# A log-softmax that streams through SBUF: eight 25 KB buffers with one maximum per row, in place of four 50 KB buffers with a maximum per piece

## The chip, the core and the metric

The kernel runs on one core of one Trainium2 chip. The metric is the device time of one execution in microseconds (us). A core has engines that run on their own and meet by semaphores: TensorE (PE in the profile), VectorE (DVE), ScalarE (ACT), GpSimd (POOL) and SyncE (SP). The last one only issues transfers here. Data moves between the device memory (HBM) and the on-chip memory SBUF (128 partitions) by 16 DMA engines, which serve the transfers that SP and ACT issue. Each issuing engine has its own queue: q1 in the profile holds the loads that SP issues, q10 the stores that ACT issues.

## The reference

The input is 16 x 512 rows of 50,000 float32 numbers, so 8,192 rows and 1,638.4 MB; the output has the same size. For each row:

```python
max_x = np.max(x, axis=-1, keepdims=True)
shifted = x - max_x
log_sum_exp = np.log(np.sum(np.exp(shifted), axis=-1, keepdims=True))
return (shifted - log_sum_exp).astype(np.float32)
```

Every number is read once, the maximum and the sum of a whole row are needed before any of its outputs can be written, and every output is written once.

## The kernel before

A row lies on G = 4 neighbouring partitions, 12,500 numbers (50,000 bytes) on each, so a tile is 32 rows on 128 partitions, 6.4 MB. There are 256 tiles and NBUF = 4 buffers of 50,000 bytes per partition; tile after tile takes the next buffer. Each engine has its own program, a loop of 64 rounds over the four buffers, and nothing but semaphores orders the engines against each other. The helper `Count` holds the value that the next instruction is to wait for; its `settle` sets a semaphore back at the end of a round; `take` (L43) waits until all 16 parts of a transfer have landed.

**SP** issues the first four loads at once (L138). After that it waits until the store out of a buffer has landed, and issues the next load into this buffer (L142).

**DVE**, for each buffer in turn: waits for the load (L43). It takes the negated maximum of each of four pieces of 3,125 numbers (L153). It then brings the four to one number per partition (L160), and spreads the maximum of the 4 partitions of a row to all of them with two 32x32 transposes and two small operations (L164 to L179). It waits for ACT, multiplies the piece sums by their corrections (L183), waits for the logarithm, and writes `x + negmax - logsum` over the buffer (L186).

**ACT**, for each buffer: exponentials of each piece, shifted by the piece's own maximum, written to a dump in PSUM with the sum of each partition kept (L201), each as soon as DVE has that piece's maximum. Then the corrections exp(piece maximum - row maximum) (L209), the logarithm of the row's sum (L215), and the issue of the store when DVE has finished the buffer (L218).

**PE** adds the corrected sums over the 4 partitions of a row by a matrix of ones and zeros, four products of one column (L229). **POOL** makes this matrix once.

So one tile goes through load, DVE, ACT, PE, ACT, DVE, store. DVE and ACT finish with one tile before they begin the next; the loads and stores of the other three buffers run meanwhile.

Of the kernel before, what the change touches and what calls it, by code (L numbers as in the profile page):

```python
# [8 lines left out]
FP32 = mybir.dt.float32  # L9
ACT = mybir.ActivationFunctionType  # L10
ALU = mybir.AluOpType
AX = mybir.AxisListType.X

P = 128
SQ = 32

G = 4
R = P // G
EXP_C = 3125
NBUF = 4  # L20


class Count:
# [11 lines left out]
    def settle(self, engine):  # L35
        if self.seen:
            engine.wait_ge(self.sem, self.seen).then_inc(self.sem, -self.seen)
        self.seen = 0


def take(engine, sem):

    engine.wait_ge(sem, 16).then_inc(sem, -16)  # L43
# [3 lines left out]
def kernel(  # L47
# [8 lines left out]
    N, V = xf.shape  # L56
    W = V // G
    assert N % R == 0 and V % G == 0 and W % EXP_C == 0
    ntiles = N // R
    nexp = W // EXP_C  # L60
    assert ntiles % NBUF == 0 and ntiles >= 2 * NBUF

    rounds = ntiles // NBUF
    xq = xf.rearrange("(q j r) (g w) -> q j (r g) w", j=NBUF, r=R, g=G)
    oq = of.rearrange("(q j r) (g w) -> q j (r g) w", j=NBUF, r=R, g=G)

    data = ctx.enter_context(tc.tile_pool(name="data", bufs=1))
    stats = ctx.enter_context(tc.tile_pool(name="stats", bufs=1))
# [7 lines left out]

    ones = consts.tile([P, P], FP32)
    bufs = [data.tile([P, W], FP32, name=f"buf{j}") for j in range(NBUF)]
    dump = dump_pool.tile([P, EXP_C], FP32, name="dump")
    rowsum = sum_pool.tile([P, NBUF], FP32, name="rowsum")  # L80

    def each(shape, name):
        return [stats.tile(shape, FP32, name=f"{name}{j}") for j in range(NBUF)]

    negms, parts, scales, scaleds = (
        each([P, nexp], n) for n in ("negm", "part", "scale", "scaled")
    )
    negmaxs, logs = each([P, SQ], "negmax"), each([P, 1], "logsum")
    negp = stats.tile([P, 1], FP32, name="negp")
    allneg = stats.tile([P, SQ], FP32, name="allneg")  # L90
    rowneg = stats.tile([P, SQ // G], FP32, name="rowneg")
    spread = stats.tile([P, SQ], FP32, name="spread")


    ctx.enter_context(tc.tile_critical())  # L95
# [1 line left out]
    def sem(name):  # L97
        return ctx.enter_context(nc.semaphore(name))

    landed = [sem(f"landed{j}") for j in range(NBUF)]  # L100
    stored = [sem(f"stored{j}") for j in range(NBUF)]
    ready = sem("ones_ready")
    on_dve = Count(sem("on_dve"))
    on_act = Count(sem("on_act"))
    shifted = Count(sem("shifted"))
    agreed = Count(sem("agreed"))
    rescaled = Count(sem("rescaled"))
    summed = Count(sem("summed"))
    added = Count(sem("added"))
    logged = Count(sem("logged"))  # L110
    subtracted = Count(sem("subtracted"))


    def dram(a, q, j):
        if isinstance(q, int):
            return a[q, j]
        return a[bass.ds(q, 1), j].rearrange("o p w -> (o p) w")
# [3 lines left out]
    @block.gpsimd  # L121
    def _(gpsimd):

        ones3 = ones.rearrange("p (r g) -> p r g", g=G)
        gpsimd.memset(ones, 1.0).then_inc(ready)  # L125
        gpsimd.affine_select(  # L126
            out=ones3, in_=ones3, pattern=[[-G, R], [0, G]], base=0,
            channel_multiplier=1, compare_op=ALU.is_ge, fill=0.0,
        ).wait_op(ready, 1, "sem-ge").then_inc(ready)
        gpsimd.affine_select(  # L130
            out=ones3, in_=ones3, pattern=[[G, R], [0, G]], base=G - 1,
            channel_multiplier=-1, compare_op=ALU.is_ge, fill=0.0,
        ).wait_op(ready, 2, "sem-ge").then_inc(ready)
# [11 lines left out]

    @block.vector
    def _(vector):
        with vector.Fori(0, rounds):
            for j in range(NBUF):
                take(vector, landed[j])  # L150

                for c in range(nexp):
                    vector.tensor_reduce(  # L153
                        out=negms[j][:, c : c + 1],
                        in_=bufs[j][:, c * EXP_C : (c + 1) * EXP_C],
                        op=ALU.max, axis=AX, negate=True,
                    ).then_inc(shifted.sem if c < nexp - 1 else on_dve.sem)
                on_dve.next(vector.nop()).then_inc(shifted.sem)  # L158

                vector.tensor_reduce(  # L160
                    out=negp, in_=negms[j], op=ALU.min, axis=AX
                ).then_inc(on_dve.sem)
                on_dve.next(
                    vector.transpose(out=allneg, in_=negp.to_broadcast([P, SQ]))  # L164
                ).then_inc(on_dve.sem)
                on_dve.next(
                    vector.tensor_reduce(  # L167
                        out=rowneg, in_=allneg.rearrange("p (r g) -> p r g", g=G),
                        op=ALU.min, axis=AX,
                    )  # L170
                ).then_inc(on_dve.sem)
                on_dve.next(
                    vector.tensor_copy(  # L173
                        out=spread.rearrange("p (r g) -> p r g", g=G),
                        in_=rowneg[:, :, None].to_broadcast([P, SQ // G, G]),
                    )
                ).then_inc(on_dve.sem)
                on_dve.next(
                    vector.transpose(out=negmaxs[j], in_=spread)  # L179
                ).then_inc(agreed.sem)  # L180

                rescaled.next(
                    vector.tensor_mul(out=scaleds[j], in0=scales[j], in1=parts[j])  # L183
                ).then_inc(summed.sem)
                logged.next(
                    vector.tensor_scalar(  # L186
                        out=bufs[j], in0=bufs[j], scalar1=negmaxs[j][:, 0:1],
                        scalar2=logs[j], op0=ALU.add, op1=ALU.subtract,
                    )
                ).then_inc(subtracted.sem)  # L190
            for count in (on_dve, rescaled, logged):
                count.settle(vector)

    @block.scalar
    def _(scalar):
        nc.scalar.preload_act_table_set("natural_log_exp_and_others")  # L196
        with scalar.Fori(0, rounds) as q:
            for j in range(NBUF):
                for c in range(nexp):
                    shifted.next(  # L200
                        scalar.activation(  # L201
                            out=dump, in_=bufs[j][:, c * EXP_C : (c + 1) * EXP_C],
                            func=ACT.Exp, bias=negms[j][:, c : c + 1], scale=1.0,
                            accum_out=parts[j][:, c : c + 1],
                        )
                    ).then_inc(on_act.sem)
                    on_act.next(scalar.nop())  # L207
                agreed.next(
                    scalar.activation(  # L209
                        out=scales[j], in_=negms[j], func=ACT.Exp,  # L210
                        bias=negmaxs[j][:, 0:1], scale=-1.0,
                    )
                ).then_inc(rescaled.sem)
                added.next(
                    scalar.activation(out=logs[j], in_=rowsum[:, j : j + 1], func=ACT.Ln)  # L215
                ).then_inc(logged.sem)
                subtracted.next(
                    scalar.dma_start(out=dram(oq, q, j), in_=bufs[j])  # L218
                ).then_inc(stored[j], 16)
            for count in (on_act, shifted, agreed, added, subtracted):  # L220
                count.settle(scalar)

    @block.tensor
    def _(tensor):
        tensor.wait_ge(ready, 3)
        with tensor.Fori(0, rounds):
            for j in range(NBUF):
                for c in range(nexp):
                    ins = tensor.matmul(  # L229
                        rowsum[:, j : j + 1], ones, scaleds[j][:, c : c + 1],  # L230
                        start=c == 0, stop=c == nexp - 1,
                    )
                    if c == 0:
                        summed.next(ins)
                ins.then_inc(added.sem)
            summed.settle(tensor)


# [28 lines left out]
```

## Time and profile before

| what | value |
|---|---|
| time of three runs | 7587.72, 7589.31 and 7597.37 us; median 7589.31 |
| the profiled execution: its own time | 7589.31 us |
| its span, first to last instruction | 7587.6 us |
| DVE busy | 5440.0 us (72%) |
| ACT busy | 3184.7 us (42%) |
| PE busy | 478.0 us (6%) |
| moved by DMA | 3276.85 MB, mean 432 GB/s |
| a load, from issue to landing (median) | 44.1 us |
| a store, from issue to landing (median) | 47.7 us |

The profile page has a row of 40 digits for each engine: the share of each fortieth of the span in which it was busy, in tenths. The DMA row does the same for the mean of the 16 DMA engines, and a row of GB/s says what they moved. Packets are the single pieces that a DMA engine moves; here a data packet is one partition's line of a tile, and a packet of 4 bytes raises the semaphore at the end of a transfer's share on one DMA engine. The trace has a record of every packet, with its queue, size, start and duration. "Chain" on the page is the work followed back from the last instruction; it knows instructions and semaphores, and not the packets of a transfer. A window view gives, for a stretch of time, the busy time of every engine, and in its last two columns the DMA share and GB/s. The landing of a transfer comes when the last of its 16 shares is done.

### The profile page before, as it was taken

Reading aid. Unit: us, or ns where it says so; the run is one execution under the profiler, and the core shown is the slowest. Engines: PE = TensorE matmul, PEld = TensorE weight load, DVE = VectorE, ACT = ScalarE, POOL = GpSimd, SP = SyncE. Lnnn points to the kernel's source line nnn. Section 1 sums busy time; section 2 is a strip of 40 time slices with the busy share of each in tenths; the row PEclk is TensorE's granted clock in tenths of the full one; section 3 lists DMA queues with packets and bytes.
Section 4 is the critical chain, followed back from the end, with each engine's and each line's share of the span. In section 5 each row is a group of like instructions: output and inputs, shape, how many; then the busy total and the mean of one; then the engine's idle time right before and its main releaser. Section 6 shows DMA issues by size and latency. Waiting matters only on the chain. (4 is left out here: it accounts for less than half of the span.)

```text
span 7587.6 us, 14087 instructions
## 1 busy us (share of the span) xinstructions
PE 478.0 (6%) x2048; PEld 456.0 (6%) x2048; DVE 5440.0 (72%) x2816; ACT 3184.7 (42%) x2561; POOL 1.4 (0%) x7
## 2 busy tenths in 40 slices
PE   0000000000000000000000000000000000000000
PEld 0000000000000000000000000000000000000000
DVE  7777777777777777777777777777777777777776
ACT  4444344443444444344443444444344443444433
POOL 0000000000000000000000000000000000000000
DMA  9999999999999999999999999999999999999998
GB/s 415 434 433 434 434 434 433 434 434 433 434 434 434 433 433 434 433 434 434 434 433 434 434 433 434 434 434 433 434 434 433 433 434 434 434 432 433 433 433 382
DMA packets 73730, 3276.85 MB, mean 432 GB/s; under 512 B 8192, under 2 KB 8192, under 8 KB 8192
## 3 DMA queue, kind: packets, MB, share of 16 engines
q1 hardware_dynamic: 36864, 1638.42, 50.0%
q10 hardware_dynamic: 36864, 1638.42, 49.9%
q14 instruction: 2, 0.02, 0.0%
HBM read 1638.40 MB, written 1638.40 MB: 432 GB/s over the span
## 5 line engine op out<-in xcount | busy, mean ns | idle before, releaser
L201 ACT ACTIVATE dump<-buf,negm 128x3125 f32<-128x3125 f32 x1024 | 2937.2, 2868 | 3802.3 <-DVE negm L153 3704.9
L153 DVE TENSOR_REDUCE negm<-buf 128x1 f32<-128x3125 f32 x1024 | 3418.2, 3400 | 920.5 <-DVEq L43 920.5
L186 DVE TENSOR_SCALAR buf<-buf,negmax,logsum 128x12500 f32<-128x12500 f32 x256 | 1738.3, 6790 | 553.8 <-ACT logsum L215 553.8
L229 PE MATMUL rowsum<-scaled,ones 128*128 128x1 f32 x2048 | 478.0, 355 | 7084.5 <-DVE scaled L183 7084.5
L229 PEld LDWEIGHTS rowsum<-scaled,ones 128*128 128x128 f32 x2048 | 456.0, 328 | 7106.4 <-DVE scaled L183 7106.4
L183 DVE TENSOR_TENSOR scaled<-scale,part 128x4 f32<-128x4 f32 x256 | 41.7, 163 | 580.5 <-ACT scale L209 580.5
L215 ACT ACTIVATE logsum<-rowsum 128x1 f32<-128x1 f32 x256 | 43.8, 171 | 551.1 <-PE rowsum L229 551.1
L201 ACT ACTIVATION_READ_ACCUMULATOR dump<-buf,negm 128x1 f32 x1024 | 190.9, 186 | 0.0
L209 ACT ACTIVATE scale<-negm,negmax 128x4 f32<-128x4 f32 x256 | 76.1, 297 | 23.6
L160 DVE TENSOR_REDUCE negp<-negm 128x1 f32<-128x4 f32 x256 | 40.1, 157 | 39.2 <-DVE negm L153 39.2
L179 DVE STREAM_TRANSPOSE negmax<-spread 128x32 f32<-128x32 f32 x256 | 54.2, 212 | 8.9
L164 DVE STREAM_TRANSPOSE allneg<-negp 128x32 f32<-128x32 f32 x256 | 54.1, 211 | 8.9
L167 DVE TENSOR_REDUCE rowneg<-allneg 128x8 f32<-128x32 f32 x256 | 47.6, 186 | 8.9
L173 DVE COPY spread<-rowneg 128x32 f32<-128x32 f32 x256 | 46.3, 181 | 8.9
L196 ACT ACT_TABLE_LOAD x1 | 1.3, 1283 | 1.0 <-SPq L95 1.0
L126 POOL TENSOR_SCALAR_AFFINE_SELECT ones<-ones 128x128 f32<-128x128 f32 x1 | 0.5, 520 | 0.1
L130 POOL TENSOR_SCALAR_AFFINE_SELECT ones<-ones 128x128 f32<-128x128 f32 x1 | 0.5, 518 | 0.1
L125 POOL MEMSET ones<- 128x128 f32 x1 | 0.2, 205 | 0.5 <-SPq L95 0.5
L251 POOL MEMSET const-bfloat16-1.0<- 128x1 bf16 x1 | 0.1, 102 | 0.0
L251 POOL MEMSET const-uint8-127<- 128x1 uint8 x1 | 0.1, 102 | 0.0
L251 POOL MEMSET const-float32-0.0<- 128x1 f32 x1 | 0.1, 99 | 0.3 <-issue 0.3
L251 POOL MEMSET const-float32-1.0<- 128x1 f32 x1 | 0.1, 99 | 0.0
## 6 DMA issues: line engine op xcount, KB each, us to landing
buf<-in_x_dram SPq DMA_DIRECT2D x256, 6250.0 KB, 44.1
out_dram<-buf ACTq DMA_DIRECT2D x256, 6250.0 KB, 47.7
```

The source lines that it names most:

```text
L153: vector.tensor_reduce(out=negms[j][:, c : c + 1], in_=bufs[j][:, c * EXP_C : (c + 1) * EXP_C], op=ALU.max, axis=AX, negate=True,).then_in ...
L160: vector.tensor_reduce(out=negp, in_=negms[j], op=ALU.min, axis=AX).then_inc(on_dve.sem)
L164: vector.transpose(out=allneg, in_=negp.to_broadcast([P, SQ]))
L167: vector.tensor_reduce(out=rowneg, in_=allneg.rearrange("p (r g) -> p r g", g=G), op=ALU.min, axis=AX,)
L173: vector.tensor_copy(out=spread.rearrange("p (r g) -> p r g", g=G), in_=rowneg[:, :, None].to_broadcast([P, SQ // G, G]),)
L179: vector.transpose(out=negmaxs[j], in_=spread)
L183: vector.tensor_mul(out=scaleds[j], in0=scales[j], in1=parts[j])
L186: vector.tensor_scalar(out=bufs[j], in0=bufs[j], scalar1=negmaxs[j][:, 0:1], scalar2=logs[j], op0=ALU.add, op1=ALU.subtract,)
L201: scalar.activation(out=dump, in_=bufs[j][:, c * EXP_C : (c + 1) * EXP_C], func=ACT.Exp, bias=negms[j][:, c : c + 1], scale=1.0, accum_out ...
L209: scalar.activation(out=scales[j], in_=negms[j], func=ACT.Exp, bias=negmaxs[j][:, 0:1], scale=-1.0,)
L215: scalar.activation(out=logs[j], in_=rowsum[:, j : j + 1], func=ACT.Ln)
L229: ins = tensor.matmul(rowsum[:, j : j + 1], ones, scaleds[j][:, c : c + 1], start=c == 0, stop=c == nexp - 1,)
```

## The change

A row lies on G = 8 partitions, 6,250 numbers (25,000 bytes) on each; a tile is 16 rows, 3.2 MB; there are 512 tiles and eight buffers of 25,000 bytes per partition, so the SBUF in use by buffers is the same. SP and POOL keep their programs, with eight in place of four in the loops (and 64 rounds still).

DVE takes one maximum of all 6,250 numbers of a partition, then the two transposes and two small operations, and hands the row's maximum to ACT. ACT takes the exponentials of two pieces of 3,125 with the row's maximum, so no corrections are needed: L209 and L183 of before are gone, with the fold at L160. PE adds two columns in place of four.

The order within DVE and ACT is another one. DVE does the front of tile j (wait for its load, maximum, spread), and then the back of tile j - 1 (the subtraction). ACT does the front of tile j (exponentials, logarithm) and then issues the store of tile j - 1. The first round stands ahead of the loop, and the last back behind it.

```diff
-G = 4
+G = 8
-NBUF = 4
+NBUF = 8
...
     @block.vector
...
+        def front(j):
+            take(vector, landed[j])
+            vector.reduce_max(out=pmax, in_=bufs[j], axis=AX).then_inc(on_dve.sem)
+
+            on_dve.next(
+                vector.transpose(out=allmax, in_=pmax.to_broadcast([P, SQ]))
+            ).then_inc(on_dve.sem)
...
+            on_dve.next(vector.transpose(out=shift[j], in_=spread)).then_inc(shifted.sem)
+
+        def back(j):
+            logged.next(
+                vector.tensor_scalar(
+                    out=bufs[j], in0=bufs[j], scalar1=shift[j][:, 0:1], scalar2=logs[j],
+                    op0=ALU.add, op1=ALU.subtract,
+                )
+            ).then_inc(subtracted.sem)
...
+        with vector.Fori(1, rounds):
+            for j in range(NBUF):
+                front(j)
+                back((j - 1) % NBUF)
+            settle()
+        back(NBUF - 1)
...
     @block.scalar
...
+        def front(j):
+            for c in range(nexp):
+                ins = scalar.activation(
+                    out=dump, in_=bufs[j][:, c * EXP_C : (c + 1) * EXP_C], func=ACT.Exp,
+                    bias=shift[j][:, 0:1], scale=1.0, accum_out=parts[j][:, c : c + 1],
+                )
+                (on_act if c else shifted).next(ins)
+                ins.then_inc(on_act.sem if c < nexp - 1 else summed.sem)
+            added.next(
+                scalar.activation(out=logs[j], in_=rowsum[:, j : j + 1], func=ACT.Ln)
+            ).then_inc(logged.sem)
+
+        def back(q, j):
+            subtracted.next(
+                scalar.dma_start(out=dram(oq, q, j), in_=bufs[j])
+            ).then_inc(stored[j], 16)
...
+        with scalar.Fori(1, rounds) as q:
+            last = q - 1
+            for j in range(NBUF):
+                front(j)
+                back(q if j else last, (j - 1) % NBUF)
+            settle()
+        back(rounds - 1, NBUF - 1)
```

More of the change, by code (lines that the diff above doesn't have):

```diff
@@ L78 @@
     bufs = [data.tile([P, W], FP32, name=f"buf{j}") for j in range(NBUF)]
+    shift = [stats.tile([P, SQ], FP32, name=f"negmax{j}") for j in range(NBUF)]
+    logs = [stats.tile([P, 1], FP32, name=f"logsum{j}") for j in range(NBUF)]
+    parts = [stats.tile([P, nexp], FP32, name=f"part{j}") for j in range(NBUF)]
+    pmax = stats.tile([P, 1], FP32, name="pmax")
+    allmax = stats.tile([P, SQ], FP32, name="allmax")
+    rowmax = stats.tile([P, SQ // G], FP32, name="rowmax")
+    spread = stats.tile([P, SQ], FP32, name="spread")
     dump = dump_pool.tile([P, EXP_C], FP32, name="dump")
     rowsum = sum_pool.tile([P, NBUF], FP32, name="rowsum")
[L82 to L92, printed above, removed]
     ctx.enter_context(tc.tile_critical())
@@ L105 @@
     shifted = Count(sem("shifted"))
-    agreed = Count(sem("agreed"))
-    rescaled = Count(sem("rescaled"))
     summed = Count(sem("summed"))
@@ L147, in _ @@
     def _(vector):
-        with vector.Fori(0, rounds):
-            for j in range(NBUF):
[L150 to L192, printed above, removed]
@@ new lines, in front @@
+        def front(j):
[4 more added lines that the diff above has]
+            ).then_inc(on_dve.sem)
+            on_dve.next(
+                vector.tensor_reduce(
+                    out=rowmax, in_=allmax.rearrange("p (r g) -> p r g", g=G),
+                    op=ALU.max, axis=AX, negate=True,
+                )
+            ).then_inc(on_dve.sem)
+            on_dve.next(
+                vector.tensor_copy(
+                    out=spread.rearrange("p (r g) -> p r g", g=G),
+                    in_=rowmax[:, :, None].to_broadcast([P, SQ // G, G]),
+                )
+            ).then_inc(on_dve.sem)
+            on_dve.next(vector.transpose(out=shift[j], in_=spread)).then_inc(shifted.sem)
@@ new lines, in back, with settle @@
+        def back(j):
[3 more added lines that the diff above has]
+                    op0=ALU.add, op1=ALU.subtract,
+                )
+            ).then_inc(subtracted.sem)
+        def settle():
+            on_dve.settle(vector)
+            logged.settle(vector)
+        for j in range(NBUF):
+            front(j)
+            if j:
+                back(j - 1)
+        settle()
@@ L194, in _ @@
+        with vector.Fori(1, rounds):
+            for j in range(NBUF):
+                front(j)
+                back((j - 1) % NBUF)
+            settle()
+        back(NBUF - 1)
     @block.scalar
     def _(scalar):
-        nc.scalar.preload_act_table_set("natural_log_exp_and_others")
-        with scalar.Fori(0, rounds) as q:
-            for j in range(NBUF):
[L199 to L221, printed above, removed]
@@ new lines, in front @@
+        def front(j):
[3 more added lines that the diff above has]
+                    bias=shift[j][:, 0:1], scale=1.0, accum_out=parts[j][:, c : c + 1],
+                )
+                (on_act if c else shifted).next(ins)
[3 more added lines that the diff above has]
+            ).then_inc(logged.sem)
@@ new lines, in back, with settle @@
+        def back(q, j):
+            subtracted.next(
+                scalar.dma_start(out=dram(oq, q, j), in_=bufs[j])
+            ).then_inc(stored[j], 16)
+        def settle():
+            for count in (on_act, shifted, added, subtracted):
+                count.settle(scalar)
+        nc.scalar.preload_act_table_set("natural_log_exp_and_others")
+        for j in range(NBUF):
+            front(j)
+            if j:
+                back(0, j - 1)
+        settle()
+        with scalar.Fori(1, rounds) as q:
+            last = q - 1
+            for j in range(NBUF):
+                front(j)
+                back(q if j else last, (j - 1) % NBUF)
+            settle()
@@ L223, in _, with add @@
+        back(rounds - 1, NBUF - 1)
     @block.tensor
     def _(tensor):
+        def add(j):
+            for c in range(nexp):
+                ins = tensor.matmul(
+                    rowsum[:, j : j + 1], ones, parts[j][:, c : c + 1],
+                    start=c == 0, stop=c == nexp - 1,
+                )
+                if c == 0:
+                    summed.next(ins)
+            ins.then_inc(added.sem)
         tensor.wait_ge(ready, 3)
@@ L227, in _ @@
             for j in range(NBUF):
[L228 to L235, printed above, removed]
+                add(j)
             summed.settle(tensor)
```

## The prediction, made before the result was known

> **What bounds the kernel now.** I read the page's DMA rows first, because DVE, the busiest engine, stands at 72%.
>
> ```profile
> DMA  9999999999999999999999999999999999999998
> ...
> DMA packets 73730, 3276.85 MB, mean 432 GB/s; under 512 B 8192, under 2 KB 8192, under 8 KB 8192
> ...
> q1 hardware_dynamic: 36864, 1638.42, 50.0%
> q10 hardware_dynamic: 36864, 1638.42, 49.9%
> ```
>
> Loads and stores together fill 99.9% of the 16 DMA engines. A queue has 256 x 128 = 32,768 data packets of 50,000 bytes and 256 x 16 = 4,096 of 4 bytes. So the kernel is bound by how fast DMA engines work through packets, and engine work matters only where it lets them run dry. The windows show where they do:
>
> ```profile
> 2000.00:3000.00 1000.00, 63.48 (x272) 60.56 (x272) 719.95 (x369) 418.23 (x337) 0.00 (x0) 1.00 1.00 434
> ...
> 7555.00:7560.00 5.00, 0.00 (x0) 0.00 (x0) 2.84 (x6) 4.59 (x4) 0.00 (x0) 1.00 0.07 30
> 7560.00:7565.00 5.00, 1.87 (x8) 1.78 (x8) 2.44 (x2) 0.47 (x2) 0.00 (x0) 1.00 0.05 20
> 7565.00:7570.00 5.00, 0.00 (x0) 0.00 (x0) 4.51 (x1) 0.00 (x0) 0.00 (x0) 1.00 0.00 0
> 7570.00:7575.00 5.00, 0.00 (x0) 0.00 (x0) 0.00 (x0) 0.00 (x0) 0.00 (x0) 1.00 1.12 480
> ```
>
> The last two columns are DMA share and GB/s. In the middle nothing is idle; at the end DMA waits for the last tile's arithmetic. A share of 0.05 is one engine of 16 (1/16 = 0.06): one lags. The timeline of DVE has that last tile:
>
> ```profile
> 7543.54 13.35 DVE L153 TENSOR_REDUCE negm<-buf 128x1 f32<-128x3125 f32 x4 [3.61 <-DVEq L43]
> ...
> 7562.72 6.79 DVE L186 TENSOR_SCALAR buf<-buf,negmax,logsum 128x12500 f32<-128x12500 f32 x1 [2.16 <-ACT logsum L215]
> ```
>
> The packet records give prices. 63,862 of the 65,536 data packets take under 1849 ns (nearly all 1847); every 4-byte packet takes 9. Inside a transfer the next packet starts 1843 to 1844 ns after the last, so neighbours overlap by some 3.5 ns; with a 4-byte packet between them it is 1849 to 1850, so that one costs 6.
>
> The lagging engine: at tile 12 its load lands 2.7 us after the median engine's, at tile 180 11.4 us, so it loses 8.7 us / 168 = 52 ns per tile. Around 2000 us its long packets (1.89 us) start at 2028.81, 2058.39, 2087.97, one per tile, each spanning SP's next load issue (2029.29, 2058.77, 2088.30). It is always last, so it sets the end.
>
> Its time must add up to the span: first packet at 2.05; 512 transfers x (8 x 1843.5 + 6 ns = 14.754 us) = 7554.0; lag 256 x 52 ns = 13.3; dry from 7565.25 (its last packet of tile 254) to 7570.38 (the last store's first packet) = 5.1; 2.3 from the last packet at 7585.3 to the end. That is 7576.8; the other 10.8 us I put on the first 100 us, where 166 of the 305 packets over 1.9 us lie.
>
> **The change part by part.**
>
> *Packets half as long: the largest term.* A line through 4 bytes/9 ns and 50,000 bytes/1847 ns has 0.03676 ns per byte and 9 ns fixed. A 25,000-byte packet then takes 9 + 919 = 928 ns, less 3.5 overlap 924.5. A transfer's share on one engine is 8 x 924.5 + 6 = 7.402 us, and 1,024 of them are 7579.6 against 7554.0: **+25.6 us**. From below: were nothing fixed per packet, only 512 more semaphore packets of 6 ns remain, +3.1. From above: no overlap and 9 ns for each, 4,096 x 9 + 512 x 9 = +41.5. I take 25.6, as both rows give it.
>
> The Trainium skill (DMA: Bandwidth & Descriptors, "Why small descriptors are slow (HBM only)") has about 3 cycles fixed per packet. At the 850 MHz that its section "Where 436 GB/s comes from" gives, that is an estimated 3.5 ns, 4,096 x 3.5 = 14.5 us, and the sum below would come out 11 us lower. The same page ("Anatomy of one DMA") speaks louder against the change: about 2.0 us fixed per DMA, by which 512 more would cost an estimated 1,024 us if nothing covered them. The packets of this trace follow each other across transfers at 1.85 us with no such hole, so I take none of it.
>
> *Twice as many load issues.* If the 52 ns hang on an issue, they double: 256 x 52 = **+13.3 us**; if on bytes or time, 0. I take 13.3, since the long packets lie on the issues.
>
> *Arithmetic, beside DMA.* DVE: from 3398 ns for 3,125 numbers and 157 for 4 (L160), 1.04 ns each; 6,250 take 6.64 us. The spread from 7557.23 to 7558.13 is 0.9, the subtraction half of 6.79 to that plus 0.16, so 3.4 to 3.55: 11.1 us a tile. ACT has two exponentials with read-out (2.87 + 0.19 each), the wait for PE (half of 1.87) and the logarithm (0.17), about 7.4. DMA needs 14.8 us per tile. The fold, the corrections, L183 and two of PE's products go; they were hidden too: nothing.
>
> *The new wait.* DVE does back(j-1) after front(j), so a finished tile waits for the next load to land; behind DVE's wait stands that subtraction, behind ACT's exponentials stands the store, and SP waits for the store to issue a load. From landing to store issue: 14.8 + 7.6 (front) + 7.4 = 29.8 us, against 26.0 before (7543.54 to 7569.54). It is two of eight buffers; 8 x 14.8 - 29.8 = 88.6 us remain for load plus store, against 44.1 + 47.7 = 91.8. Both queues stay about three transfers deep: nothing. If the cover were gone: see the third rival.
>
> *The end.* After the last landing L, the store before last is issued at L + 7.6 + 7.4 = L + 15, the last one 3.5 later. Before, the lagging engine had stores until L + 21.8 (7543.4 to 7565.25). With as much left it doesn't run dry: **-5.1 us**. With nothing left, 15 us dry: +10.
>
> *The beginning.* The first load is half as long and the first store is issued near 33.5 us (two fronts of DVE after a landing near 11, then ACT's 7.4) instead of 45.38, so loads resume before the first ones run out. Of the 10.8 us that may save none (the slow packets come from the first mixing of reads and writes) or all. I take half, **-5 us**.
>
> **Sum:** 7587.6 + 25.6 + 13.3 - 5.1 - 5 = 7616.4 of span; with the 1.7 between this execution's span and its own time (7589.31, which is also the median) 7618 us, 0.38% slower. This kernel's runs tell about 0.2%, 15 us, from no change.
>
> **The rivals.** *Lag by time* (chance 0.22): the lag doesn't double. 7618 - 13.3 = 7605, on the edge of the 15 us. For it: the lagging engine may simply be slow.
>
> *No fixed cost per packet* (0.13; the one on the other side): packets go by bytes alone, and the shorter ends decide. 7589.3 + 3.1 - 5.1 - 5 to -10.8 = 7576 to 7582. It decides if a packet's fixed cost is under (10.1 - 3.1) / 4,096 = 1.7 ns and the lag stays. For it: 3.5 of the 9 ns overlap already; against it: the 5.5 that don't.
>
> *The store's wait starves the queues* (0.05): each us by which load plus store need more than the 88.6 costs 1/8 us per tile, 64 us in all. Against it: a store alone in its queue, the last one, took 7587.6 - 7569.54 = 18 us for twice the bytes.
>
> *Dearer small packets* (0.12): the full 9 ns or more for starts that lie otherwise in memory: 7618 + 16 = 7634 and, at 15 ns, 7660.
>
> *The forecast's own case* has 0.48. That the change does not do what it says has no room: the shapes are set by two constants.
>
> **How the numbers follow.** Slower by over 0.2% means above 7604.5: the forecast's case nearly whole, half of the lag rival, the two dear ones: 0.74. Faster means below 7574: the end of the second rival, 0.04. Within: 0.22. Range 7588 to 7642: it leaves out most of the second rival and the dear ones' upper parts.
>
> **What would show it.** Right: DMA share 1.00 and a rate near 432 GB/s in the middle windows (3.2 MB x 2 / 14.8 us), packets of 928 ns, a lag growing by 50 ns per tile, no dry window before the last store. Wrong: packets of 924 ns or less (second rival), a lag that ends near 13 us (first), shares under 1.00 in the middle (third), packets over 935 (fourth).

## The result and the profile after

The changed kernel takes 7618.68 us (median of six runs, 7617.30 to 7620.36), the kernel before 7589.23 us (median of six, 7587.59 to 7597.37). The ratio is 1.0036 with a 95% interval of 1.0023 to 1.0049: 29 us slower, beyond what these runs scatter. Runs more than 1.5% above the fastest of their kernel, two of loads_in_two and one of before_no_pe, are left out of the times given below. The prediction was 7618 us. The profiled execution of the changed kernel took 7619.4 us with a span of 7617.7, so 30.1 us more span than before.

The page of the changed kernel, its DMA rows:

```profile
span 7617.7 us, 14954 instructions
...
DMA  9999999999999999999999999999999999999998
GB/s 424 432 433 432 432 432 432 433 432 432 432 433 433 432 432 432 433 432 432 432 432 433 432 432 432 433 433 432 431 432 433 432 432 432 432 432 432 431 430 366
DMA packets 147459, 3276.88 MB, mean 430 GB/s; under 512 B 16385, under 2 KB 16385, under 8 KB 16385
...
q1 hardware_dynamic: 73728, 1638.43, 50.0%
q10 hardware_dynamic: 73728, 1638.43, 50.0%
```

The bytes are the same and the packets twice as many. The queues fill the DMA engines as before, and in the middle the rate is 432 where it was 434 GB/s. The bound is still DMA; it moves the same data a little more slowly.

Its groups of instructions, DVE's two big ones (the last columns are busy time, mean ns of one, and idle time before them with its releaser):

```profile
L143 DVE TENSOR_REDUCE pmax<-buf 128x1 f32<-128x6250 f32 x512 | 3411.5, 6663 | 1960.6 <-DVEq L43 1960.6
...
L164 DVE TENSOR_SCALAR buf<-buf,negmax,logsum 128x6250 f32<-128x6250 f32 x512 | 1789.4, 3495 | 3.9 <-ACT logsum L197 3.9
```

The maximum took 6.66 us (worked out: 6.64), the subtraction 3.50 (3.4 to 3.55). Of the time that DVE waits for something, all but 3.9 us is for a landing, and only the last subtraction waits for a logarithm. So the arithmetic is hidden.

The end, in windows (last two columns: DMA share and GB/s):

```profile
2000.00:3000.00 1000.00, 67.92 (x268) 62.19 (x268) 731.86 (x404) 416.33 (x338) 0.00 (x0) 1.00 1.00 432
...
7560.00:7565.00 5.00, 0.00 (x0) 0.00 (x0) 3.90 (x4) 4.38 (x3) 0.00 (x0) 1.00 0.23 100
...
7575.00:7580.00 5.00, 0.00 (x0) 0.00 (x0) 3.81 (x3) 4.51 (x3) 0.00 (x0) 1.00 0.24 100
...
7595.00:7600.00 5.00, 1.01 (x4) 0.93 (x4) 2.34 (x1) 1.52 (x3) 0.00 (x0) 1.00 0.42 180
7600.00:7605.00 5.00, 0.00 (x0) 0.00 (x0) 1.19 (x1) 0.00 (x0) 0.00 (x0) 1.00 1.00 430
```

Before, one window had a share of 0.00. Here the share falls to 0.23 again and again over 40 us and never to nothing. Fifteen engines have run out of loads and get one store every 15 us; one engine still has its own loads to do. By the packet records that engine has no hole at all between 7500 us and its last packet's end at 7615.83; the others are empty for some 25 us of it. The timeline says what they wait for:

```profile
7582.70 6.66 DVE L143 TENSOR_REDUCE pmax<-buf 128x1 f32<-128x6250 f32 x1 [3.87 <-DVEq L43]
7582.72 0.34 ACTq L202 DMA_DIRECT2D out_dram<-buf  x1
...
7597.59 3.98 ACTq L202 DMA_DIRECT2D out_dram<-buf  x2
```

The last load landed at 7582.6, some 38 us after the median engine had finished its share of it (7544.8). The store before last went out 15.0 us after this landing (worked out: 15), the last one 3.6 us later (the group of two is 3.98 us long; worked out: 3.5).

### The profile page after: what moved, and what is told of

The parts are those of the page before. It is cut to its first block, busy times and chain, and to the rows that moved or that the text cites. A ratio compares the mean times of both kernels' runs of the same rounds, so it can differ in the third digit from the quotient of the medians.

```text
span 7617.7 us, 14954 instructions
## 1 busy us (share of the span) xinstructions
PE 519.0 (7%) x2048; PEld 475.1 (6%) x2048; DVE 5565.8 (73%) x3072; ACT 3153.3 (41%) x2561; POOL 1.2 (0%) x7
## 5 line engine op out<-in xcount | busy, mean ns | idle before, releaser
L143 DVE TENSOR_REDUCE pmax<-buf 128x1 f32<-128x6250 f32 x512 | 3411.5, 6663 | 1960.6 <-DVEq L43 1960.6
L190 ACT ACTIVATE dump<-buf,negmax 128x3125 f32<-128x3125 f32 x1024 | 2938.2, 2869 | 3878.6 <-DVE negmax L160 3862.1
L164 DVE TENSOR_SCALAR buf<-buf,negmax,logsum 128x6250 f32<-128x6250 f32 x512 | 1789.4, 3495 | 3.9 <-ACT logsum L197 3.9
L227 PE MATMUL rowsum<-part,ones 128*128 128x1 f32 x2048 | 519.0, 357 | 7078.5 <-ACT dump L190 7078.5
L227 PEld LDWEIGHTS rowsum<-part,ones 128*128 128x128 f32 x2048 | 475.1, 322 | 7122.2 <-ACT dump L190 7122.2
L190 ACT ACTIVATION_READ_ACCUMULATOR dump<-buf,negmax 128x1 f32 x1024 | 190.8, 186 | 0.0
L160 DVE STREAM_TRANSPOSE negmax<-spread 128x32 f32<-128x32 f32 x512 | 108.3, 212 | 17.7
L146 DVE STREAM_TRANSPOSE allmax<-pmax 128x32 f32<-128x32 f32 x512 | 108.3, 211 | 17.6
L149 DVE TENSOR_REDUCE rowmax<-allmax 128x4 f32<-128x32 f32 x512 | 95.1, 186 | 17.7
L155 DVE COPY spread<-rowmax 128x32 f32<-128x32 f32 x512 | 92.5, 181 | 17.8
## 6 DMA issues: line engine op xcount, KB each, us to landing
buf<-in_x_dram SPq DMA_DIRECT2D x512, 3125.0 KB, 51.8
```

Of the source, the lines that this page charges most:

```text
L143: vector.reduce_max(out=pmax, in_=bufs[j], axis=AX).then_inc(on_dve.sem)
L146: vector.transpose(out=allmax, in_=pmax.to_broadcast([P, SQ]))
L149: vector.tensor_reduce(out=rowmax, in_=allmax.rearrange("p (r g) -> p r g", g=G), op=ALU.max, axis=AX, negate=True,)
L155: vector.tensor_copy(out=spread.rearrange("p (r g) -> p r g", g=G), in_=rowmax[:, :, None].to_broadcast([P, SQ // G, G]),)
L160: on_dve.next(vector.transpose(out=shift[j], in_=spread)).then_inc(shifted.sem)
L164: vector.tensor_scalar(out=bufs[j], in0=bufs[j], scalar1=shift[j][:, 0:1], scalar2=logs[j], op0=ALU.add, op1=ALU.subtract,)
```

## The experiments

Each kernel was timed against the kernel before on its chip. The kernel before scattered more there than in the first runs (7584.5 to 7632 us over 48 runs, medians 7592.9, 7589.4 and 7594.4), so a few us are read from the packet records and not from medians. Two numbers from them return. The *landing period* is the mean time from one tile's landing to the next as DVE sees it, which is the lagging engine's pace; the *lag* is this less what an undisturbed engine needs for a tile by 1843.5, 924.5 or 465 ns per packet and 6 ns per semaphore. For before, the landing period is 29.560 us (first three quarters) and the lag 29.560 - 29.508 = 52 ns a tile; for the changed kernel 14.868 - 14.804 = 64 ns.

### Half packets alone: packets_cut

```diff
-    bufs = [data.tile([P, W], FP32, name=f"buf{j}") for j in range(NBUF)]
+    bufs = [data.tile([P, H, half + PAD], FP32, name=f"buf{j}") for j in range(NBUF)]
+    body = [b[:, :, 0:half] for b in bufs]
```

(in the kernel before; H = 2, PAD = 8 numbers)

> The kernel before with one thing changed: each buffer has a gap of 32 bytes in its middle, so a partition's 50,000 bytes go as two packets of 25,000, with the tiles, the transfers, the load issues and the order of the work as before. If a packet has a fixed cost as the forecast has it (924.5 ns from start to start), a tile takes an engine 2 x (16 x 924.5 + 6 ns) = 29.596 us in place of 29.508, +22.6 us over 256 tiles: 7612 us. If packets go by bytes alone: 7589 us. The lag of the last engine stays at 52 ns per tile by either theory on it, since neither issues nor PE's work change.

7605.67 us (7605.07 to 7611.46, ten runs), ratio 1.0008 with an interval of 0.9996 to 1.0021: the timing alone doesn't prove a loss, though the lowest of its ten runs is above the median of before, 7592.9. Its page:

```profile
DMA packets 139266, 3276.85 MB, mean 431 GB/s; under 512 B 8192, under 2 KB 8192, under 8 KB 8192
...
q1 hardware_dynamic: 69632, 1638.42, 50.1%
q10 hardware_dynamic: 69632, 1638.42, 50.0%
```

Twice the data packets, and no more semaphore packets than before. A packet takes 928 ns, as forecast, and an undisturbed engine passes a tile in 29.603 us (29.507 before): 256 x 96 ns = +24.6 us against +22.6 expected. The landing period is 29.678, so the lag grew too, from 52 to 82 ns a tile (75 by the engine's own 29.603), where either theory expected 52. The span grew by 21.1 us only: over the whole run the landing period is 29.677 us against 29.572, which is 27 us, and the first 100 us went some 6 us better than in the run before. So the fixed cost of a packet is there without any other part of the change, and it is the largest part of the loss.

### A third size on the line: g16

```diff
-G = 8
+G = 16
-NBUF = 8
+NBUF = 16
```

> The changed kernel with G = 16 and sixteen buffers of 12,500 bytes: the line through the two packet sizes goes on. A packet of 12,500 bytes takes 9 + 459.5 = 468.5 ns, 465.0 from start to start; 1,024 tiles x (16 x 465.0 + 12 ns = 7.452 us) = 7630.8 us on a DMA engine, against 7579.6 for 25,000 bytes. With a lag of 45 to 61 ns per tile (the lower without half of PE's share, as PE makes one product per tile) 46 to 62 us come on top, and 7 us of ends: 7684 to 7700 us. If packets go by bytes and only the lag doubles: 7630 to 7650 us. DVE (6.3 us) and ACT (some 4 us) stay under the 7.45 us of a tile.

7688.78 us (7672.9 to 7697.3), ratio 1.0116 (1.0089 to 1.0142); expected 7684 to 7700.

```profile
DMA packets 294916, 3276.96 MB, mean 426 GB/s; under 512 B 32768, under 2 KB 32768, under 8 KB 32768
...
L143 DVE TENSOR_REDUCE pmax<-buf 128x1 f32<-128x3125 f32 x1024 | 3489.5, 3408 | 1403.6 <-DVEq L43 1403.6
```

DVE still waits for landings, so DMA is the bound. A packet of 12,500 bytes takes 468 ns, on the line through 4 and 50,000 bytes (468.5). The landing period is 7.504 us, the lag 7.504 - 7.452 = 52 ns a tile. With the same data in 256, 512 and 1,024 tiles the lag per tile is 52, 64 and 52 ns: it goes with the tile and not with the byte. The tile is not the whole of it: packets_cut has 82 ns with 256 tiles.

### What the lag hangs on: loads_in_two, no_pe, pe_twice

```diff
+        for lo in (0, P // 2):
+            part = slice(lo, lo + P // 2)
+            sync.dma_start(out=bufs[j][part], in_=dram(xq, q, j)[part]).then_inc(landed[j], 16)
```

(in the kernel before)

> The kernel before with each load issued as two transfers of 64 partitions: 512 load issues in place of 256, packets of 50,000 bytes, the rest as before. If the last engine's lag hangs on a load issue (the forecast's step), it goes from 52 to 104 ns per tile, +13.3 us, and 256 more semaphore packets of 6 ns add 1.5: 7604 us. The rival is that it hangs on PE's products, since in both traces the long packets gather around them: then the lag stays at 52 ns per tile and the time is 7591 us.

9742 us (9741 and 9743): neither theory. Loads of 64 partitions are a bad instrument: half the data packets take over 2.05 us, where 1.85 was usual, and the rate fell to 336 GB/s. It says nothing on the lag.

```diff
-            added.next(
-                scalar.activation(out=logs[j], in_=rowsum[:, j : j + 1], func=ACT.Ln)
+            on_act.next(
+                scalar.activation(out=logs[j], in_=parts[j][:, 0:1], func=ACT.Ln)
...
-        with tensor.Fori(0, rounds):
-            for j in range(NBUF):
-                add(j)
-            summed.settle(tensor)
```

(in the changed kernel; the logarithm waits for ACT's own sum instead of PE's)

> The changed kernel without PE's products: the logarithm is taken of the first partial sum of each partition, so the sum over pieces and partitions is left out. Load issues, packets and order stay. If the lag hangs on load issues: 61 ns per tile as before it, 7618 us. If it hangs on PE's products, the part of it outside them is all that stays, some 10 ns per tile: 512 x 50 ns = 26 us less, 7592 us.

7603.6 us (7603.17 to 7608.79, ten runs): 15 us under the changed kernel, whose six runs lie between 7617.3 and 7620.4. The landing period is 14.835, the lag 31 ns a tile in place of 64. Packets more than 3% over their usual time went from 655 to 115, half of these in the first 100 us. With the load issues untouched, half of the lag and nearly all long packets are gone; the forecast's cause, the load issue, explains at most the other half. The edit also starts the logarithm some 1.1 us earlier, as nothing is left to wait for; the next run moves it the other way.

```diff
+            for c in range(nexp):
+                ins = tensor.matmul(
+                    rowsum[:, j : j + 1], ones, parts[j][:, c : c + 1],
+                    start=c == 0, stop=c == nexp - 1,
+                )
```

(in the changed kernel, behind the same products into other columns)

> The changed kernel with PE's products of each tile made twice, the first time into columns that nobody reads; the second microsecond of PE work lies beside DVE's work. If the lag hangs on load issues: unchanged, 7618 us. If it hangs on PE's products and on how long they last: up to twice the 61 ns per tile, +31 us, 7649 us; if on their beginning alone: 7618 us with a lag of 61 ns.

7644.25 us, but from 7620.7 to 7653.7. The GB/s row of the profiled run shows why it scatters:

```profile
GB/s 425 432 432 432 432 433 431 433 431 433 431 433 432 433 432 433 432 433 432 433 431 433 432 433 432 432 432 432 432 431 432 432 428 424 423 423 423 422 422 363
```

For four fifths of the span it is the changed kernel's rate, then it drops by 2%, and packets of all engines get longer there. Before the drop the lag is 14.875 - 14.804 = 71 ns a tile, against 64. So twice the products, and a logarithm some 0.9 us later, add 7 ns, not 61: it is not how long PE works. By that, 3.6 of the 26 us above the changed kernel are lag (512 x 7 ns); most of the rest comes with the late drop, whose cause the run doesn't show. The fastest of the six runs, 7620.7, lies 2 us over the changed kernel.

### The same questions on the kernel before: one_column, before_no_pe

```diff
+                on_dve.next(
+                    vector.tensor_reduce(
+                        out=totals[j], in_=scaleds[j], op=ALU.add, axis=AX
+                    )
+                ).then_inc(summed.sem)
...
-                        rowsum[:, j : j + 1], ones, scaleds[j][:, c : c + 1],
+                        rowsum[:, j : j + 1], ones, totals[j], start=True, stop=True
```

> The kernel before with the four corrected sums added on DVE (one more small reduction, some 0.2 us a tile), so PE makes one product per tile in place of four; DVE's and PE's work is hidden behind DMA. If PE's products make the long packets: the lag goes from 52 ns per tile to some 35, 4 to 6 us less than the kernel before, 7584 us. If the lag hangs on load issues: unchanged, 7589 us.

7608.5 us, from 7576.3 to 7673.6; interval of the ratio 0.9989 to 1.0062. Inconclusive in time: three of the ten runs lie near 7576, the lowest seen here and some 8 us under every run of the kernel before, while the profiled one, of 7648.6, has a late drop as pe_twice. Before its drop the lag is 29.572 - 29.508 = 64 ns a tile, so in that execution a quarter of PE's products does not lower it; PE's share, if it is one, would then be paid once per tile. What made the three fast is not shown: a smaller lag in them is not ruled out.

> The kernel before without PE's products: the logarithm is taken of the first corrected sum of each partition, so the sum over pieces and partitions is left out. If PE's products make the long packets, as in the changed kernel without them: hardly a packet above 1.86 us in the middle, a lag of some 30 ns per tile or less, 6 us less, 7583 us. If the lag hangs on load issues: 52 ns per tile and 7589 us.

It drops PE's products as no_pe does, in the kernel before. 7619.2 us (median of nine runs, 7584.5 to 7646.3), ratio 1.0026 (1.0008 to 1.0044): not faster, but slower by 0.3%. The profiled run has 2,613 long packets, nearly all loads, from the first to about 6200 us, on all engines alike; after that there is hardly one, and the landing period is 29.51 us. That is the pace of the engine that lands last, and there it is another one that loses time: by the landings of its shares it falls from 0.7 to 3.4 us behind the first engine between tiles 212 and 254, while the others keep 29.508. So without PE's products one engine still loses some 65 ns a tile, no less than with them, and more than no_pe would lead one to expect. It is one stretch of one execution; up to 6200 us, what the run was to show lies under the long packets.

### More load issues, with all partitions: cut_two_issues, extra_issue

```diff
+        for h in range(H):
+            sync.dma_start(out=body[j][:, h], in_=halves(xq, q, j)[:, h]).then_inc(landed[j], 16)
```

(in packets_cut)

> The kernel with its packets cut, and each load issued as two transfers, one for each half of the columns: all 128 partitions take part in each, so the 16 DMA engines get the same packets as without this edit, and only the load issues (512 in place of 256) and 4,096 more packets of 4 bytes are added. If the lag hangs on load issues: from 83 to some 130 to 165 ns per tile (29.679 us from landing to landing there, less 29.596), so 12 to 21 us more, 7618 to 7627 us after 7605.7. If it doesn't: 256 x 6 ns for the semaphores, 7607 us.

7656.67 us (7648 to 7700), 51 us over packets_cut and not 1 or 12 to 21. The landing period is 29.96 us, and the median engine has nearly the same, 29.95: all 16 slowed down, and none falls further and further behind the others. The five runs fall into two groups, 7648 to 7657 and 7695 to 7700; the profiled one (7694.7) is of the second, so the records show the worse case.

```diff
+                take(sync, extra[j])
                 sync.dma_start(out=bufs[j], in_=dram(xq, q, j)).then_inc(landed[j], 16)
+                sync.dma_start(out=scraps[j], in_=xq[0, 0, 0:16, 0:8]).then_inc(extra[j], 16)
```

(in the changed kernel)

> The changed kernel with a second load issue of SP behind each load: 16 lines of 32 bytes into a scrap tile, one on each DMA engine, which nobody reads. Every DMA engine gets one short packet and one semaphore packet more per tile, some 15 to 20 ns, 8 to 10 us in all. If the lag hangs on load issues (the step on record): another 61 ns per tile, +31 us on top, 7660 us. If it doesn't: 7618.7 + 8 to 10 = 7628 us, and the lag of the last engine behind the others stays near 61 ns per tile.

7750.28 us (7726.9 to 7758.8), 132 us over the changed kernel, so 257 ns for each added load of 512 bytes; both expectations of the time fail. The landing period is 15.12 us, the median engine's 15.05. No single engine falls behind 15 others that keep together, as in the changed kernel: all 16 are slower and drift apart, to some 50 us between the first landing of a load's shares and the last (at most 60; 39 in the changed kernel). At the end the last engine is 31 us behind the median one, against 38, so this distance did not double. The long packets went from 655 to 8,046, most of them loads. Its issues, with the median time to landing (51.8 and 37.0 us in the changed kernel):

```profile
buf<-in_x_dram SPq DMA_DIRECT2D x512, 3125.0 KB, 71.8
out_dram<-buf ACTq DMA_DIRECT2D x512, 3125.0 KB, 18.7
```

So a second load issue per tile is dear, but by another way than the forecast's: it comes with longer load packets on every engine, not with one long packet on the last.

### The order without the size, and the size without the order

old_order_25k is the kernel before with G = 8 and NBUF = 8, new_order_50k the changed one with G = 4 and NBUF = 4.

> The order and the piece maxima of before, with G = 8 and eight buffers of 25,000 bytes: so the half-size tiles without the new order. DVE finishes a tile before it begins the next: two piece maxima 6.7 us, the spread 1.06, the wait for the corrections 2.27 with the product, the wait for PE and the logarithm some 1.25, the subtraction 3.5, and waits between: 15.1 us a tile, over the 14.87 that DMA needs. 512 x 15.1 = 7731, with ends 7760 us, and DMA shares under 1.00 in the middle. If DVE hides it, as the forecast's text said of all arithmetic: 7618 us as the changed kernel.

7774.87 us (7774.7 to 7778.9), ratio 1.0237 (1.0220 to 1.0255). The landing period is 15.147 us (worked out: 15.1). Its waits, a window of its middle, and its issues with the median time to landing:

```profile
DVE scaled L183 <- ACT scale L209: 1155.6, 512, 2.3
DVE buf L186 <- ACT logsum L215: 671.5, 512, 1.3
...
DVE negm L153 <- DVEq L43: 11.3, 1, 11.3
```

```profile
2000.00:3000.00 1000.00, 66.89 (x264) 61.23 (x264) 744.17 (x595) 426.59 (x397) 0.00 (x0) 1.00 1.00 422
```

```profile
buf<-in_x_dram SPq DMA_DIRECT2D x512, 3125.0 KB, 18.3
out_dram<-buf ACTq DMA_DIRECT2D x512, 3125.0 KB, 18.1
```

DVE waits once for a landing, the first. Everywhere else the data is there before DVE is, and DVE stands 1155.6 + 671.5 us waiting for ACT within a tile. DVE's chain is the bound. Only the share misled the expectation: it says 1.00, as packets lengthened when there was no hurry (5,739 long ones, with 142 us of extra time per engine).

> The changed kernel's order with G = 4 and four buffers of 50,000 bytes. A finished tile waits for the next load: from its landing to its store one tile period P, then DVE's front 14.3 us and ACT's 14.4. Four periods are P + 28.7 + load + store. With both transfers at half rate (29.5 + 3.3 us each) P would be 31.4 us, 8040 us in all; if the queues overlap better, P goes down to DMA's 29.56 and the time to that of before with a longer end, 7600 us. By the theory that this wait is hidden at any depth of buffers: 7600 us; by the buffer count: 7700 to 8050 us with DMA shares under 1.00.

8132.01 us (8127 to 8166), ratio 1.072 (1.069 to 1.075): the buffer count decides, and at more than was worked out (P = 31.73 us in place of 31.4, and 82 us over the 8050 that bounded the time).

```profile
2000.00:3000.00 1000.00, 58.48 (x251) 55.83 (x252) 644.02 (x187) 385.94 (x287) 0.00 (x0) 1.00 0.99 403
```

```profile
DVE pmax L143 <- DVEq L43: 2780.3, 254, 19.1
```

```profile
buf<-in_x_dram SPq DMA_DIRECT2D x256, 6250.0 KB, 32.3
out_dram<-buf ACTq DMA_DIRECT2D x256, 6250.0 KB, 32.6
```

DVE waits for landings again, 2780.3 us in all, and a load is in flight for 32.3 us where it was 44.1 before: one transfer per queue and no second one behind it. The wait that the new order adds costs nothing with eight buffers and 543 us with four (8132.0 - 7589.2).

## Why the prediction was right, point by point

The sum, term by term, from the packet records of the two profiled executions:

| term (whole run) | forecast, us | measured, us | from |
|---|---|---|---|
| packets half as long | +25.6 | +27.4 | 512 x 14.807 - 256 x 29.507, the median engine's tile |
| lag of the last engine | +13.3 | +15.1 | 512 x (14.868 - 14.807) - 256 x (29.570 - 29.507) |
| dry at the end | -5.1 | -5.1 | no hole on the lagging engine |
| beginning | -5 | -6.9 | what is left: 8.3 us before, 1.4 after |
| last packet to end of span | 0 | -0.4 | 1.9 against 2.3 us |
| span | +28.8 | +30.1 | |

**Packets.** Right in mechanism and size. The packets take the 928 ns that the line gave, and packets_cut and g16 show it without the rest of the change. The rival without a fixed cost is out: by it packets_cut had no reason for packets over 923.5 ns. So is the dearer one, which wanted over 935.

**Lag.** The size was right, the step behind it was not. The forecast hung the 52 ns on SP's load issue, because three long packets lay on three issues. What the runs show: 52 to 64 ns per tile at three tile sizes, so doubling with the tiles was right. That the term came out is luck as far as its cause goes, for whatever happens once per tile doubles. With PE's products gone and every load issue in place, it falls from 64 to 31 ns, and nearly all long packets vanish. The three issues of the forecast also lay within 1 us of PE's products, and I did not look at a stretch where the two come apart: in the kernel before, around 314 us, the long packet (314.2 to 316.1) lies on PE's products and SP's issue comes after it, where around 2029 us it lay on both:

```profile
315.31 1.86 PE L229 MATMUL rowsum<-scaled,ones 128*128 128x1 f32 x8 [27.69 <-DVE scaled L183]
...
317.81 0.33 SPq L142 DMA_DIRECT2D buf<-in_x_dram  x1
```

```profile
2029.29 0.33 SPq L142 DMA_DIRECT2D buf<-in_x_dram  x1
...
2029.89 1.87 PE L229 MATMUL rowsum<-scaled,ones 128*128 128x1 f32 x8 [27.70 <-DVE scaled L183]
```

The packet records say the same of longer stretches. From 300 to 3600 us the time by which packets run over their usual time adds up to 53 ns a tile before and 61 after, which is the lag; 28 of the 53 and 39 of the 61 lie on packets that end within 2 us of the start of PE's products. Behind SP's load issue the bulk has no fixed place: 0 to 4 us before, 6 to 8 in the changed kernel, 3 to 5 in pe_twice. So most of it does not follow the load issue. That PE's products do is not shown either: twice the products add 7 ns, in the one execution that shows it a quarter of them takes nothing off, and the quiet stretch of before_no_pe has the whole lag without them. What makes one engine lose time once per tile stays open, and so do the 31 ns of no_pe; more load issues did not tell, as they slowed every engine.

**The new wait.** Right that it costs nothing here; the in-flight times moved as this view says, with their sum of 88.8 us against 88.6 worked out:

```profile
buf<-in_x_dram SPq DMA_DIRECT2D x512, 3125.0 KB, 51.8
out_dram<-buf ACTq DMA_DIRECT2D x512, 3125.0 KB, 37.0
```

The two queues were not equally deep, as the text had them (three and a half loads, two and a half stores). new_order_50k shows that the cover is the count of buffers.

**Arithmetic beside DMA.** Right for the new order: DVE is busy for 10.9 us a tile (5565.8 / 512; worked out: 11.1) of 14.87. The forecast named DVE's time only in the new order; old_order_25k shows that the same small tiles in the old one would have made DVE the bound and cost 186 us over the kernel before. So the order pays for what the size would lose, and what is left to see is the price of the packets.

**The end and the beginning.** The lagging engine does not run dry, as forecast. The beginning shows in one window of each kernel, before and after:

```profile
0.00:100.00 100.00, 5.60 (x24) 5.35 (x24) 66.45 (x34) 38.59 (x31) 1.45 (x7) 1.00 0.99 399
```

```profile
0.00:100.00 100.00, 7.10 (x28) 6.50 (x28) 82.55 (x47) 47.22 (x38) 1.21 (x7) 1.00 0.99 419
```

At 433 GB/s, 20 GB/s more for 100 us are 4.6 us. The first store went out at 33.52 us (worked out: 33.5), and long packets in this stretch fell from 166 to 50 packets.

The rule of the Trainium skill (DMA: Bandwidth & Descriptors, "Why small descriptors are slow (HBM only)") with its 3 cycles per packet, an estimated 3.5 ns, would have given 14.5 us for the data packets. The forecast set that against its whole 25.6 and came to 11 us less, but the 25.6 also holds 3.1 us of semaphore packets; with these the page's estimate is 17.6 us, 8 under the forecast and 10 under the 27.4 measured. The runs have some 5 ns per packet beyond the bytes (924.5 - 25,000 x 0.03676 = 5.5), against these 3.5. The page's 2.0 us per DMA ("Anatomy of one DMA") stand there under the path for transfers that GpSimd issues, and here SP and ACT issue them. They do not add up over the transfers of this case, which queue behind each other: 512 more cost 29 us in all.

## What to carry to other kernels

Where two queues keep the DMA engines full, price a change by packets: fit a line through two packet sizes of the trace, and multiply by their number; it held to 2 us over 131,072 packets here. Follow the engine that lands last and not the mean, for it sets the end. When long records coincide with one event, look for a stretch of the trace where that event and its neighbours come apart before naming it the cause. And a DMA share of 1.00 does not prove that DMA is the bound: ask whether the first compute engine ever waits for a landing.

## What the runs showed of the hardware that was not expected

- A DMA share of 1.00 at 422 GB/s beside a DVE that waits for the first landing only (old_order_25k), and 1.00 at 434 GB/s in the kernel before: a packet that lengthens fills the share as well.
- Stretches in which packets of all engines run long and the rate drops by 1 to 8%: the first 100 us of before (399 GB/s), the last fifth of pe_twice and one_column, the last three eighths of g16 (430 to 426 GB/s), nearly the whole of cut_two_issues, extra_issue, old_order_25k and new_order_50k. Whether the engines keep step does not decide it: a load's shares land within 9 us of each other in old_order_25k and new_order_50k, and up to 60 us apart in extra_issue. In those last four a store is in flight for 34.6, 18.7, 18.1 and 32.6 us, little over what a transfer takes at half the rate (29.5, 14.8, 14.8 and 29.5), so hardly a store waited behind another. That this lengthens packets would fit; no run tested it.
- A load of 512 bytes behind each load of 3.2 MB cost 257 ns per tile, more than ten times the 18 ns that its two packets take on an engine (9 each).
- Loads of 64 partitions in place of 128, with the same packets, lowered the rate from 432 to 336 GB/s.
